# Seven beginnings within a 64-byte line for the split weights of a two-block network on one core

## The chip, the core and the metric

The kernel runs on one core of a Trainium2 chip. The metric is device time in microseconds (us) of one execution, all weights being read from HBM; the run before was timed three times.

## The reference

Two networks run one after the other on 256 tokens of width 1024, in float32. The first has four layers (a gated mixer with a causal convolution of 31 taps, an attention with 16 heads and forget gates, a mixer with a convolution of 3 taps, and the first kind again). The second has two layers, each with a two-branch attention and a feed-forward part of width 2 x 2816. What matters here is that nearly all of the work has this form:

```python
def conv_ffn(h, w_up, conv_w, conv_b, w_down):
    u = h @ w_up
    ...
    return (jax.nn.silu(g) * val) @ w_down
```

A matrix of activations (256 tokens) is multiplied by a large matrix of weights that is used once. The other mixers (`h @ w_in`, `... @ w_out`) are the same product with other nonlinear steps between.

## The kernel before, in words

**Weights.** A weight matrix comes in tiles of 128 x 1024 float32 (512 KB). `need` (L684, called for every tile) starts the DMA into a buffer `wr` and then makes two tiles of it: ScalarE writes `wh`, the value rounded to the type fp32r, and VectorE writes `wl = wr - wh`, the rest. Activations are split in the same way, into `hh` and `hl` (eight chunks of 128 x 256, kept for a layer) or into `ph` and `pl` (one chunk each).

**Products.** `mm3` makes one float32 product from three matmuls in fp32r: `wh` by `hh`, `wh` by `hl`, `wl` by `hh`. The weights are the stationary operand (128 x 128, a LDWEIGHTS of its own before each matmul), the activations the moving one (256 columns). `dense` does this for eight chunks into half a PSUM bank `pd`, `pair` for two such halves; `Out` accumulates the second matrix of a mixer into four banks `po`. `tokens512` turns the operands round: there `wh` and `wl` move (512 columns) and the activations stay. Tiles of the kind "native" are not split: they are multiplied from `wr` in plain float32.

**Order.** `Graph.schedule` plays the whole program through with costs for each instruction, and writes down on which engine and in which order everything is issued. It also gives each buffer its slot: five for `wr`, six for `wh`, seven for `wl`, in rotation. `place` (L467 to L481) then makes the tile of a slot; every tile is padded to a multiple of 128 bytes (LINE), and three small unused tiles (PHASES) set off the pools.

**Addresses.** In the built program the pools lie so that every tile begins 32 bytes into a 64-byte line of SBUF: `hh` at byte 29856 of each partition, `wr0` at 64608, `wh0` at 85088, `wl0` at 89184, `ph0` at 197024, and all other slots a multiple of 64 bytes behind these. A slice of 128 columns of weights, or of one chunk of activations, is 512 or 1024 bytes further, so each LDWEIGHTS and each matmul begins at 32 within its line, too.

Of the kernel before, what the change touches and what calls it, by code (L numbers as in the profile page):

```python
# [18 lines left out]
LINE = 128  # L19

PHASES = {"const": 8, "weights": 16, "big": 16}
WIDTH = {F32: 4, F32R: 4, I32: 4, BF: 2}
DEBUG = []

# [100 lines left out]
class Graph:  # L125
# [341 lines left out]
    def place(self, pool, b, tag):  # L467

        size = WIDTH[b.dtype]
        n, line = int(np.prod(b.shape[1:])), LINE // size  # L470
        if b.pool == "psum" or n % line == 0:
            return pool.tile(b.shape, b.dtype, name=b.name, tag=tag, bufs=1)
        t = pool.tile([b.shape[0], -(-n // line) * line], b.dtype, name=b.name, tag=tag, bufs=1)[:, :n]
        names = [f"a{i}" for i in range(len(b.shape) - 1)]
        if len(names) == 1:
            return t
        return t.rearrange(f"p ({' '.join(names)}) -> p {' '.join(names)}", **dict(zip(names[1:], b.shape[2:])))


    def issue(self, tc, ctx, pools):  # L480
        nc = tc.nc  # L481
        ctx.enter_context(tc.manual_schedule())
        made = {n: ctx.enter_context(tc.tile_pool(name=n, bufs=1, **kw)) for n, kw in pools.items()}
        for n, w in PHASES.items():
            made[n].tile([128, w], F32, name="phase_" + n, tag="phase", bufs=1)
# [1363 lines left out]
```

## Time and profile before

| | |
|---|---|
| time, median of 3 runs | 1811.41 us (1805.84 to 1814.57) |
| profiled execution: its own time | 1812.58 us |
| profiled execution: its span | 1810.8 us |
| TensorE matmul busy | 1792.4 us (99%) |
| TensorE weight load busy | 1722.9 us (95%) |
| VectorE busy | 1483.2 us (82%) |
| ScalarE busy | 1102.9 us (61%) |
| GpSimd busy | 363.6 us (20%) |
| DMA, mean rate | 185 GB/s |

Matmuls overlap, and a matmul's duration in the trace (280 ns) is the time from its start until its result is there. The pace of a row of matmuls is read from their starts, not from their durations: in the chain of waits, where a piece gives the count of matmuls and the time that they took together, or in the timeline, which gives the start of each.

### The profile page before, as it was taken

Reading aid. Unit: us, or ns where it says so; the run is one execution under the profiler, and the core shown is the slowest. Engines: PE = TensorE matmul, PEld = TensorE weight load, DVE = VectorE, ACT = ScalarE, POOL = GpSimd, SP = SyncE. Lnnn points to the kernel's source line nnn. Section 1 sums busy time; section 2 is a strip of 40 time slices with the busy share of each in tenths; the row PEclk is TensorE's granted clock in tenths of the full one; section 3 lists DMA queues with packets and bytes.
Section 4 is the critical chain, followed back from the end, with each engine's and each line's share of the span. In section 5 each row is a group of like instructions: output and inputs, shape, how many; then the busy total and the mean of one; then the engine's idle time right before and its main releaser. Section 6 shows DMA issues by size and latency. Waiting matters only on the chain.

```text
span 1810.8 us, 37129 instructions
## 1 busy us (share of the span) xinstructions
PE 1792.4 (99%) x14088; PEld 1722.9 (95%) x14088; DVE 1483.2 (82%) x3264; ACT 1102.9 (61%) x1975; POOL 363.6 (20%) x462
## 2 busy tenths in 40 slices
PE   9999999999999999999999999999999999999998
PEld 8999998999999999999999989999999989999998
DVE  7999998777787777689998897889998675687676
ACT  6786665554554444477767469665556468765554
POOL 3997311000010000069953000010001000000001
PEclk9999999999999999999999999999999999999999
DMA  6445666776747655444465756658884433446561
GB/s 219 151 139 188 187 217 197 254 250 226 241 146 223 177 174 174 152 128 142 151 196 184 238 175 204 207 177 279 274 271 127 163 126 119 136 157 209 187 187 48
DMA packets 107171, 334.90 MB, mean 185 GB/s; under 512 B 12784, under 2 KB 13168, under 8 KB 106992
## 3 DMA queue, kind: packets, MB, share of 16 engines
q1 hardware_dynamic: 106992, 332.52, 57.1%
q8 instruction: 111, 1.82, 0.4%
q14 instruction: 68, 0.56, 0.1%
HBM read 331.43 MB, written 1.05 MB: 184 GB/s over the span
## 4 chain that ended last, share of the span: by engine, by line
PE 88%; DVE 6%; DMA 3%; ACT 2%; issue 1%; POOL 0%; SPq 0%; ACTq 0%; DVEq 0%; POOLq 0%
PE pd L512 59%; PE po L512 21%; PE pa L512 8%; DMA wa<-in_w_ada 2%; DVE wl L512 1%; PE idle L512 1%; DVE wa L512 1%; ACT L512 0%; ACT wh L512 0%; DVE x L512 0%; DMA wr<-in_a_in 0%; DVE hn L512 0%; DVE IQ L512 0%; DVE hh L512 0%; DVE nm L512 0%
## 5 line engine op out<-in xcount | busy, mean ns | idle before, releaser
L512 ACT ACTIVATE wh<-wr 128x1024 fp32r<-128x1024 f32 x466 | 489.4, 1056 | 401.1 <-PE pd L512 257.0
L512 DVE TENSOR_TENSOR wl<-wr,wh 128x1024 fp32r<-128x1024 f32 x466 | 574.9, 1241 | 126.9 <-ACT wh L512 124.4
L512 PE MATMUL pd<-hh,wh 128*128 128x256 f32 x2360 | 670.0, 286 | 3.0 <-DVE up L512 2.1
L512 PE MATMUL pd<-hl,wh 128*128 128x256 f32 x2360 | 660.8, 283 | 0.2 <-DVE hl L512 0.2
L512 PE MATMUL pd<-hh,wl 128*128 128x256 f32 x2360 | 660.2, 283 | 0.0
L512 PEld LDWEIGHTS pd<-hh,wh 128*128 128x128 f32 x2360 | 445.5, 189 | 5.8 <-ACT wh L512 2.0
L512 PEld LDWEIGHTS pd<-hl,wh 128*128 128x128 f32 x2360 | 443.1, 189 | 1.6 <-issue 0.5
L512 PEld LDWEIGHTS pd<-hh,wl 128*128 128x128 f32 x2360 | 443.4, 189 | 1.2 <-issue 0.5
L512 POOL TENSOR_TENSOR C<-C,tap 128x230 f32<-128x230 f32 (+16 forms) x366 | 269.0, 758 | 47.0 <-ACT tap L512 35.2
L512 PE MATMUL po<-ph,wh 128*128 128x256 f32 x904 | 250.4, 282 | 0.0
L512 PE MATMUL po<-ph,wl 128*128 128x256 f32 x904 | 249.2, 281 | 0.0
L512 PE MATMUL po<-pl,wh 128*128 128x256 f32 x904 | 238.6, 281 | 0.1
L512 DVE SCALAR_TENSOR_TENSOR po<-U,vec,po 128x255 f32<-128x255 f32 (+19 forms) x530 | 216.4, 471 | 2.2
L512 PE MATMUL pd<-hn,wr 128*128 128x256 f32 x960 | 214.7, 381 | 0.0
L512 PEld LDWEIGHTS pd<-hn,wr 128*128 128x128 f32 x960 | 179.8, 190 | 23.0
L512 PEld LDWEIGHTS po<-ph,wh 128*128 128x128 f32 x904 | 169.8, 188 | 0.7 <-ACT ph L512 0.3
L512 PEld LDWEIGHTS po<-ph,wl 128*128 128x128 f32 x904 | 170.1, 188 | 0.0
L512 ACT ACTIVATE tap<-U,vec 128x226 f32<-128x226 f32 (+17 forms) x366 | 155.3, 479 | 17.3 <-POOL C L512 8.1
L512 PEld LDWEIGHTS po<-pl,wh 128*128 128x128 f32 x904 | 162.8, 188 | 0.4 <-DVE pl L512 0.3
L512 POOL TENSOR_TENSOR sq<-sq 128x256 f32<-128x256 f32 x16 | 13.6, 850 | 443.7 <-ACT sq L512 443.1
L512 POOL TENSOR_TENSOR r<-r,neghalf 128x4 f32<-128x4 f32 (+1 forms) x22 | 28.8, 1309 | 298.4 <-DVE r L512 258.4
L512 DVE CUSTOM_DVE_ANT_0 wa<-wa,scr,mods 128x512 f32<-128x512 f32 x96 | 72.1, 751 | 14.1 <-DMA wa<-in_w_ada 13.5
(272 smaller groups left out, 2502.1 us busy)
## 6 DMA issues: line engine op xcount, KB each, us to landing
wr<-in_a_in SPq DMA_DIRECT2D x96, 512.0 KB, 3.6
wa<-in_w_ada SPq DMA_DIRECT2D x192, 256.0 KB, 3.8
wr<-in_w_up SPq DMA_DIRECT2D x88, 512.0 KB, 4.3
wr<-in_c_in SPq DMA_DIRECT2D x64, 512.0 KB, 3.6
wr<-in_m_in SPq DMA_DIRECT2D x64, 512.0 KB, 4.3
wr<-in_b_in SPq DMA_DIRECT2D x48, 512.0 KB, 4.5
wr<-in_w_dn SPq DMA_DIRECT2D x44, 512.0 KB, 4.2
wr<-in_a_out SPq DMA_DIRECT2D x32, 512.0 KB, 4.4
```

The lines of the kernel that those rows point to most:

```text
L512: getattr(eng[o.eng], o.fn)(*args, **kw)
```

## The change

`place` gives the slots of `wh` and `wl` a beginning of their own. A table SHIFT names the number of float32 elements by which the tile's first element is moved behind the slot's first byte: 8, 10, 12, 14, 2, 4 for the six slots of `wh`, and the same with a 6 at the end for the seven slots of `wl`. The slot itself becomes 128 bytes longer, so the slot that follows begins at 32 within its line again.

```diff
+SHIFT = {"wh": (8, 10, 12, 14, 2, 4), "wl": (8, 10, 12, 14, 2, 4, 6)}
...
-        if b.pool == "psum" or n % line == 0:
+        turn = SHIFT.get(b.tag)
+        at = turn[b.slot % len(turn)] if turn else 0
+        if b.pool == "psum" or n % line == 0 and not at:
             return pool.tile(b.shape, b.dtype, name=b.name, tag=tag, bufs=1)
-        t = pool.tile([b.shape[0], -(-n // line) * line], b.dtype, name=b.name, tag=tag, bufs=1)[:, :n]
+        t = pool.tile([b.shape[0], -(-(n + at) // line) * line], b.dtype, name=b.name, tag=tag, bufs=1)[:, at:at + n]
```

In the built program the tiles begin at these bytes of a 64-byte line:

| slot | 0 | 1 | 2 | 3 | 4 | 5 | 6 |
|---|---|---|---|---|---|---|---|
| `wh`, before | 32 | 32 | 32 | 32 | 32 | 32 | |
| `wh`, changed | 0 | 8 | 16 | 24 | 40 | 48 | |
| `wl`, before | 32 | 32 | 32 | 32 | 32 | 32 | 32 |
| `wl`, changed | 0 | 8 | 16 | 24 | 40 | 48 | 56 |

All other tiles (`wr`, `hh`, `hl`, `ph`, `pl`, x and the rest) still begin at 32. No instruction is added, dropped or moved: on each of the five engines the list of instructions, with what each waits for, is the same as before but for the line numbers, and each slot holds the same tiles.

## Rows read from the trace of the kernel before

**Rows 1.** The page: busy time by engine; granted clock in 40 slices; the chain's shares.

```profile
PE 1792.4 (99%) x14088; PEld 1722.9 (95%) x14088; DVE 1483.2 (82%) x3264; ACT 1102.9 (61%) x1975; POOL 363.6 (20%) x462
...
PEclk9999999999999999999999999999999999999999
...
PE 88%; DVE 6%; DMA 3%; ACT 2%; issue 1%; POOL 0%; SPq 0%; ACTq 0%; DVEq 0%; POOLq 0%
PE pd L512 59%; PE po L512 21%; PE pa L512 8%; DMA wa<-in_w_ada 2%; DVE wl L512 1%; PE idle L512 1%; DVE wa L512 1%; ACT L512 0%; ACT wh L512 0%; DVE x L512 0%; DMA wr<-in_a_in 0%; DVE hn L512 0%; DVE IQ L512 0%; DVE hh L512 0%; DVE nm L512 0%
```

**Rows 2.** Matmul groups: out<-moving,stationary, shapes, count, busy us, mean ns, idle before.

```profile
L512 PE MATMUL pd<-hh,wh 128*128 128x256 f32 x2360 | 670.0, 286 | 3.0 <-DVE up L512 2.1 <-ACT hh L512 0.8
...
L512 PE MATMUL po<-ph,wh 128*128 128x256 f32 x904 | 250.4, 282 | 0.0
...
L512 PE MATMUL po<-hh,wh 128*128 128x256 f32 x184 | 51.3, 279 | 0.0
...
L512 PE MATMUL pd<-wh,hh 128*128 128x512 f32 x80 | 32.7, 411 | 0.0
...
L512 PE MATMUL pd<-ph,wh 128*128 128x256 f32 x72 | 21.2, 295 | 1.2 <-DVE qm L512 0.8 <-ACT hn L512 0.2
```

**Rows 3.** Chain in both feed-forward parts: start us, us, what, count.

```profile
1246.48 5.65 PE pd L512 x48
1252.14 2.83 PE po L512 x24
...
1638.30 5.65 PE pd L512 x48
1643.95 2.83 PE po L512 x24
```

**Rows 4.** Chain from 942 us, output matrix of the fourth layer.

```profile
942.30 8.28 PE po L512 x72
...
950.71 34.06 PE po L512 x300
```

**Rows 5.** Timeline of TensorE around 988 us: start us, duration us, matmul.

```profile
987.78 0.28 PE L512 MATMUL pd<-hl,wh 128*128 128x256 f32 x1
...
988.12 0.28 PE L512 MATMUL pd<-hl,wh 128*128 128x256 f32 x1
...
989.04 0.28 PE L512 MATMUL pd<-hh,wl 128*128 128x256 f32 x1
...
989.40 0.28 PE L512 MATMUL pd<-hh,wl 128*128 128x256 f32 x1
```

**Rows 6.** Timeline of weight loads: eight for matmuls of one column.

```profile
1015.85 0.97 PEld L512 LDWEIGHTS pa<-cst,sq 128*128 128x128 f32 x8
```

**Rows 7.** Busy us (and count) by stretch: PE, PEld, DVE, ACT, POOL, clock, DMA.

```profile
945.00:975.00 30.00, 30.00 (x268) 29.96 (x267) 29.95 (x49) 21.16 (x34) 13.20 (x12) 1.00 0.69 207
1240.00:1350.00 110.00, 110.00 (x937) 110.00 (x936) 101.70 (x203) 62.89 (x91) 0.00 (x0) 1.00 0.87 281
...
1640.00:1760.00 120.00, 120.00 (x1021) 120.00 (x1020) 84.92 (x128) 66.23 (x100) 0.00 (x0) 1.00 0.60 188
```

**Rows 8.** Timeline: first and last of 18 matmuls with 512 moving columns.

```profile
239.01 0.40 PE L512 MATMUL pd<-wh,rawl 128*128 128x512 f32 x1
...
243.21 0.40 PE L512 MATMUL pd<-wh,rawl 128*128 128x512 f32 x1
```

**Rows 9.** Groups of VectorE and ScalarE, columns as in rows 2.

```profile
L512 DVE TENSOR_TENSOR wl<-wr,wh 128x1024 fp32r<-128x1024 f32 x466 | 574.9, 1241 | 126.9 <-ACT wh L512 124.4 <-DMA wr<-in_w_b 0.4
...
L512 DVE SCALAR_TENSOR_TENSOR y<-u,vec,y 128x255 f32<-128x255 f32 x16 | 7.7, 484 | 0.5
L512 DVE SCALAR_TENSOR_TENSOR y<-u,vec,y 128x254 f32<-128x254 f32 x16 | 7.7, 483 | 0.5
...
L512 ACT ACTIVATE tap<-U,vec 128x226 f32<-128x226 f32 x32 | 15.1, 472 | 0.5 <-DVE U L512 0.2 <-POOL C L512 0.2
...
L512 ACT ACTIVATE tap<-U,vec 128x236 f32<-128x236 f32 x16 | 7.6, 478 | 0.0
```

## The prediction

> **What bounds the kernel now.** I read the page first. TensorE is busy for 99% of the span at the full clock (every slice of the clock line is a 9), and the chain of waits lies on TensorE for 88%: 59% on `pd`, 21% on `po` [rows 1]. So the pace of the matmuls is the time, and everything else feeds it. The groups tell which matmuls these are. There are 2360 + 904 + 184 + 72 = 3520 triples of fp32r matmuls with 256 moving columns and split weights, 10,560 in all [rows 2] (each row is one of three with the same count).
>
> Next comes their pace. In both feed-forward parts the chain repeats one piece: 48 matmuls into `pd` in 5.65 us, 24 into `po` in 2.83 us [rows 3]. That is 8.48 us for 72, or 117.8 ns from start to start, alike at 1246 us and at 1638 us. VectorE is busy for 101.7 of 110 us in the first of these stretches and for 84.9 of 120 in the second, and DMA engines for 0.87 and 0.60 of the time [rows 7]; the pace does not move with it. 10,560 x 117.8 ns = 1244 us is 69% of the span, nearly the whole of the chain's share on `pd` and `po` less the unsplit tiles.
>
> The row that matters most is the exception. In the output matrix of the fourth layer 300 such matmuls take 34.06 us, 113.5 ns each [rows 4], while VectorE is busy for 29.95 of 30 us [rows 7]. The fast pace ends at 988.2 us with no idle time: three matmuls take 0.34 us just before (987.78 to 988.12), and 0.36 us soon after (989.04 to 989.40) [rows 5], the same kind of matmul on buffers that all begin at byte 32. So at equal addresses there are two stable paces, 113.5 and 117.8 ns, 4.3 ns apart, and what decides is how the streams of TensorE happen to stand to each other in time. I put the matmuls at the fast pace at some 700 (400 from 942 to 988 us, the rest in pieces of 10 to 90), so 9,860 go at the slow one.
>
> A third row gives a floor. Eight weight loads for matmuls of one column take 0.97 us together, the last 0.19 us of it its own duration [rows 6]: (0.97 - 0.19) / 7 = 111.4 ns from load to load. No split matmul can go faster, because each brings a load of the same 128 columns.
>
> **The change part by part.** No instruction and no wait is added, so the change can only alter durations. There are four places where it could.
>
> *Weight loads* (two in three from `wh`, one in three from `wl`). All 10,560 matmuls load from a tile whose beginning moves against that of the moving tile, by seven amounts, and never by none. The trace has no load that begins elsewhere than at 32, so its cost is bounded from both sides. Best, every matmul goes at the floor: 117.8 - 111.4 = 6.4 ns on 9,860 and 2.1 ns on 700, 65 us. The nearest row on that side is the fast pace: 9,860 x 4.3 ns = 42 us. Worst, I allow one step of the same size upward, since 4.3 ns is the only step that the trace shows: 10,560 x 4.3 ns = 45 us lost. I take the middle between the two measured paces, 2.15 ns on 9,860, 21 us gained. The reason is that the slow pace is a standing that returns to itself triple after triple while all beginnings are alike. Now `wh` and `wl` rotate through six and seven beginnings, so the standing differs from tile to tile (every 8 triples), and the two known paces are what it can fall into. Why not all at the fast pace: a standing that suits one beginning need not suit the next.
>
> *Matmuls with moving weights.* Of these there are 240 in the shape of rows 2, and 48 more. Eighteen take 4.20 us, 233.3 ns each [rows 8]. Twice the step above would be 288 x 8.6 ns = 2.5 us either way; I take 0.
>
> *Splitting.* VectorE and ScalarE now write and read tiles that begin elsewhere: 466 subtractions of 1241 ns [rows 9] and as many copies. Instructions whose operands begin 4 or 8 bytes further are there: 255 elements in 484 ns and 254 in 483; on ScalarE 226 elements in 472 ns and 236, begun 40 bytes earlier in the row, in 478 [rows 9]. This is 0.6 to 1 ns per element and no step at any beginning, so I take 0. Were it 5 ns on each of the 466 pairs, it would be 2.3 us on each engine, hidden where VectorE has 35 of 120 us free, not in the stretch from 945 us where it has none [rows 7].
>
> *Longer slots.* 13 x 128 bytes push `wa` and the pools behind; all still begin at 32, so 0.
>
> How much of a faster pace reaches the end? In the second feed-forward part all of it: VectorE has 84.9 of 120 us of work. In the first it has 101.7 of 110 us, 92%; a pace 4% faster still leaves TensorE last. Around 945 us VectorE is full. In the convolution layers short waits between matmuls will take some. I count 0.9 of the gain: 21 x 0.9 = 19 us. The sum against the profiled execution is 1812.6 - 19 = 1793.6 us. That execution is 1.2 us above the median of the three runs, so against the median it is 1792; I say 1793.
>
> **Rivals.**
>
> *All at the fast pace or below.* If equal beginnings are what makes the slow standing possible, it vanishes: 42 x 0.9 = 38 us, 1774; with the floor as the end, 65 us, 1747. For it: one stretch of 300 holds the fast pace over 12 tiles. Against it: that stretch shows that equal beginnings do not exclude the fast pace, so they are not the whole cause.
>
> *The places do not matter.* Two paces at equal addresses can be read as a proof that addresses are not the cause: the standing is set by the last interruption, and so it stays. Then the slow pace keeps its 117.8 ns, and the time is 1811, with 9 us either way for the luck of the interruptions. The Trainium skill, "SBUF — State Buffer", section on the two separate sides, says that TensorE's port waits for no other engine. The rows agree (the same 117.8 ns under light and heavy VectorE load), but two streams of TensorE itself are not other engines. By that rule the change is worth nothing.
>
> *Slower.* A load that begins at an odd multiple of 8 bytes may cost more. This holds for three of six `wh` slots and four of seven `wl` slots, so for 2/3 x 3/6 + 1/3 x 4/7 = 52% of the loads. The place is the load under the running matmul, the price one step of 4.3 ns: 0.52 x 10,560 x 4.3 ns = 24 us, 1836. With all seven it is 45 us, 1858. It decides as soon as the load ends after the matmul that covers it; with 111.4 ns from load to load against 117.8 the room is 6.4 ns, and at the fast pace only 2.1 ns. For it: so little room. Against it: no row shows a dearer beginning on any engine. The Trainium skill, "SBUF — State Buffer", specifications, speaks against the change here: SBUF is read in lines of 16 bytes, and each crossing into a new line costs. A load begun in mid-line crosses one line more; no run here shows that.
>
> **How the numbers follow.** Half a step faster (1793): 0.36. Fast pace everywhere or below (1747 to 1780): 0.11. No effect (1802 to 1820): 0.25. Slower (1820 to 1858): 0.28. Hence faster by over 0.5% 0.46 (0.01 of the first case falls short of it), same 0.26, slower 0.28; 0.5%, 9 us, is about what a measurement of this kernel can tell from no change. The likeliest case alone spans 1778 to 1802. Leaving out half of the second case and a little over a third of the last gives 1768 to 1838 for 8 in 10.
>
> **What would show it.** The chain's pieces of 48 and 24 in the feed-forward parts: 5.55 and 2.77 us in the forecast, with differing pieces from tile to tile; 5.45 and 2.72 at the fast pace throughout; 5.65 and 2.83 if nothing happens; over 5.75 if the odd beginnings cost. The subtraction should stay at 1241 ns. The forecast is wrong if the pace within one tile's 24 matmuls leaves the band from 113 to 118 ns, or if the pace falls and the span does not, because VectorE then sets the end.

## The result, and the profile after

The changed kernel takes 1816.59 us (median of nine runs, 1814.04 to 1818.68), the kernel before in the same runs 1807.54 us (1801.2 to 1814.57). The ratio is 1.0054 (95% interval 1.0031 to 1.0077): slower by half a per cent, where 1793 us and a gain were forecast. The time lies in the range of 1768 to 1838 us; the direction is wrong.

The page after: busy time by engine, and the shares of the chain of waits by engine.

```profile
span 1816.1 us, 37129 instructions
...
PE 1801.2 (99%) x14088; PEld 1733.4 (95%) x14088; DVE 1483.4 (82%) x3264; ACT 1103.0 (61%) x1975; POOL 362.2 (20%) x462
...
PEclk9999999999999999999999999999999999999999
...
PE 91%; DVE 4%; DMA 3%; ACT 1%; issue 1%; POOL 0%; SPq 0%; ACTq 0%; DVEq 0%; POOLq 0%
```

Against [rows 1] TensorE's times have moved: 1792.4 to 1801.2 us of matmuls and 1722.9 to 1733.4 us of weight loads. VectorE (1483.2 to 1483.4) and ScalarE (1102.9 to 1103.0) stand still. The medians differ by 9 us. The two profiled executions, 1812.58 and 1817.94 us, differ by less: the span grows by 5.3 us (1810.8 to 1816.1), the matmul time by 8.8 us, and 3.5 us of TensorE's idle time are gone (18.4 to 14.9 us), as the chain's share on VectorE falls from 6 to 4%. No engine waits for something new; the matmuls have a slower pace.

The clock has to be looked at, too. A 9 in the clock line means 90% or more of a slice, so it is not the full clock throughout, as the prediction read it. One stretch of the kernel before, columns as in [rows 7]:

```profile
1000.00:1006.00 6.00, 6.00 (x29) 6.00 (x30) 2.27 (x6) 0.69 (x1) 1.80 (x1) 0.50 0.96 336
```

Here the granted clock is 0.50, the lower of its two levels (1.2 GHz). Apart from the program's last 15 us there are four such stretches before, 20 us together, and six after, 27 us; elsewhere it is 1.00 (2.4 GHz). Of the 7 us more at half clock at most half, 3.4 us, can be time lost in the profiled execution after. The clock is not the result, though: over the runs it is the same on the mean, 0.993 in the nine of the change and in the 31 of the kernel before that were timed beside pad_only, and the paces below are taken without the triples at half clock.

The chain of the second feed-forward part and of the fourth layer's output matrix after: start us, us, what, count.

```profile
942.68 8.65 PE po L516 x72
...
951.46 35.59 PE po L516 x300
...
1633.66 5.69 PE pd L516 x48
1639.35 2.84 PE po L516 x24
1642.19 5.67 PE pd L516 x48
1647.86 2.83 PE po L516 x24
1650.69 5.71 PE pd L516 x48
1656.39 2.83 PE po L516 x24
```

Two things have changed. Where before nearly every piece was 5.65 and 2.83 us [rows 3], the pieces now differ from tile to tile and lie a little above: here 5.67 to 5.71 and 2.83 to 2.84, in the first feed-forward part 5.61 to 5.70 and 2.82 to 2.88. And the fast stretch of [rows 4], 300 matmuls in 34.06 us, takes 35.59 us, 118.6 ns each: the fast pace is gone.

The same can be said of all matmuls with split weights. I took the starts of every triple of them with nothing between (9,715 in each trace) and left out some 260 with a wait or at half clock. Before, 7.5% of the triples took 342 ns or less (the fast pace, 113.3 ns a matmul) and the others 117.79 ns a matmul, on the mean 117.45. After, 0.1% are fast and the mean is 118.16. The difference on 10,560 matmuls, 0.71 ns each, is 7.5 us. Half of it (0.075 x 10,560 x 4.9 ns = 3.9 us) is the fast pace that ended, the other half (0.925 x 10,560 x 0.37 ns = 3.6 us) a dearer slow pace. Each share is that of one profiled execution; the one before lies above the median of its kernel (1812.58 against 1807.54 us), so its usual share of the fast pace may be larger, which no run shows.

The groups of the split after: count, then busy us and mean ns of one, and idle time before.

```profile
L516 DVE TENSOR_TENSOR wl<-wr,wh 128x1024 fp32r<-128x1024 f32 x466 | 575.3, 1242 | 129.0 <-ACT wh L516 125.0 <-DMA wr<-in_b_v 0.8 <-DMA wr<-in_w_a 0.4
...
L516 ACT ACTIVATE wh<-wr 128x1024 fp32r<-128x1024 f32 x466 | 490.6, 1059 | 405.1 <-PE pd L516 253.5 <-PE po L516 71.7 <-issue 51.8
```

The subtraction takes 1242 ns against 1241 [rows 9], the copy 1059 against 1056 in the trace before: on the mean, VectorE and ScalarE do not mind where the tile begins.

### The profile page after: what moved, and what is told of

Its sections match the earlier page's. It is cut to its first block, busy times and chain, and to the rows that moved or that the text cites. A ratio compares the mean times of both kernels' runs of the same rounds, so it can differ in the third digit from the quotient of the medians.

```text
span 1816.1 us, 37129 instructions
## 1 busy us (share of the span) xinstructions
PE 1801.2 (99%) x14088; PEld 1733.4 (95%) x14088; DVE 1483.4 (82%) x3264; ACT 1103.0 (61%) x1975; POOL 362.2 (20%) x462
## 4 chain that ended last, share of the span: by engine, by line
PE 91%; DVE 4%; DMA 3%; ACT 1%; issue 1%; POOL 0%; SPq 0%; ACTq 0%; DVEq 0%; POOLq 0%
PE pd L516 59%; PE po L516 22%; PE pa L516 8%; DMA wa<-in_w_ada 2%; PE idle L516 1%; DVE wl L516 1%; DVE wa L516 1%; DMA wr<-in_b_in 1%; DMA wr<-in_a_in 0%; ACT wh L516 0%; DVE IQ L516 0%; DVE nm L516 0%; DVE x L516 0%; DVE hd L516 0%; DVE m L516 0%
## 5 line engine op out<-in xcount | busy, mean ns | idle before, releaser
L516 ACT ACTIVATE wh<-wr 128x1024 fp32r<-128x1024 f32 x466 | 490.6, 1059 | 405.1 <-PE pd L516 253.5
L516 DVE TENSOR_TENSOR wl<-wr,wh 128x1024 fp32r<-128x1024 f32 x466 | 575.3, 1242 | 129.0 <-ACT wh L516 125.0
```

The lines of the kernel that those rows point to most:

```text
L516: getattr(eng[o.eng], o.fn)(*args, **kw)
```

## Experiments

Each kernel was timed beside runs of the kernel before on the same chip; ratios are to these. "Pace" is the mean over the triples described above, "fast" the share of triples at 342 ns or less. Two measures of a place are needed. One is the byte at which a tile begins in its 64-byte line, 32 in the kernel before. The other is the distance: how far the moving tile (`hh`, `hl`, `ph`, `pl`) begins behind the weights, counted within 256 bytes. In the kernel before all weights begin at 96 within 256 bytes and all moving tiles at 160, so every distance is 64. All kernels have the same instructions (14,088 matmuls each); only addresses differ. Their mean granted clock lies between 0.9915 and 0.9942; the slowest kernel, d0, has the highest and mix_all64, one of the three fastest, the lowest, so the clock does not order them.

| kernel | ratio (95%) | pace, ns | fast |
|---|---|---|---|
| before | 1 | 117.45 | 7.5% |
| the change | 1.0054 (1.0031 to 1.0077) | 118.16 | 0.1% |
| pad_only | 0.9964 (0.9945 to 0.9982) | 116.46 | 38.5% |
| wh_only | 1.0060 (1.0032 to 1.0087) | 118.17 | 0.1% |
| wl_only | 1.0027 (1.0011 to 1.0042) | 117.57 | 2.7% |
| all_0 | 1.0063 (1.0042 to 1.0084) | 118.43 | 0% |
| all_40 | 1.0043 (1.0024 to 1.0063) | 118.20 | 0% |
| all_48 | 1.0023 (1.0005 to 1.0042) | 117.87 | 0% |
| shift_256 | 1.0012 (0.9992 to 1.0031) | 117.82 | 0% |
| d0 | 1.0124 (1.0090 to 1.0158) | 119.89 | 0% |
| d128 | 1.0076 (1.0053 to 1.0100) | 118.93 | 0% |
| d192 | 0.9936 (0.9906 to 0.9966) | 115.36 | 53.8% |
| mix | 0.9849 (0.9812 to 0.9886) | 113.74 | 90.6% |
| mix_seven | 1.0067 (1.0047 to 1.0087) | 118.42 | 0% |
| mix_w16 | 1.0088 (1.0057 to 1.0119) | 118.84 | 0% |
| mix_all16 | 1.0020 (1.0000 to 1.0040) | 117.69 | 1.4% |
| mix_all32 | 0.9863 (0.9832 to 0.9893) | 113.76 | 90.2% |
| mix_all64 | 0.9884 (0.9857 to 0.9911) | 113.78 | 89.9% |

### The longer slots alone

```diff
-SHIFT = {"wh": (8, 10, 12, 14, 2, 4), "wl": (8, 10, 12, 14, 2, 4, 6)}
+SHIFT = {"wh": (0,) * 6, "wl": (0,) * 7}
...
-        if b.pool == "psum" or n % line == 0 and not at:
+        if b.pool == "psum" or n % line == 0 and not turn:
...
-... [b.shape[0], -(-(n + at) // line) * line] ...
+... [b.shape[0], (-(-(n + at) // line) + (1 if turn else 0)) * line] ...
```

This is pad_only: the slots stay 128 bytes longer, nothing is shifted in them.

> The slots of wh and wl are 128 bytes longer, as in the change, but nothing is shifted: all tiles begin at 32 within their 64-byte line. Theory A (what costs is that the beginnings differ from slot to slot): the two paces of before, 117.8 and 113.3 ns, and nothing between; 1803 to 1812 us. Theory C (the distance between the slots costs, not the beginning within the line): a spread of paces around 118.2 ns as in the changed kernel, and 1813 to 1819 us.

1803.79 us, 0.4% faster than before: in theory A's range, though not with its two paces alone. Chain of the second feed-forward part in this kernel, and its output matrix of the fourth layer.

```profile
946.71 34.06 PE po L516 x300
...
1620.93 5.70 PE pd L516 x48
1626.63 2.73 PE po L516 x24
1629.37 5.68 PE pd L516 x48
1635.04 2.73 PE po L516 x24
```

The pieces into `po` run at the fast pace (2.73 / 24 = 113.8 ns), those into `pd` slower than before (5.70 / 48 = 118.8). All tiles still begin at 32 within the line, but the distances have changed. Each `wl` but the last of the seven now lies 128 bytes off its `wh` within 256, and 13 x 128 = 1664 = 6.5 x 256 bytes push `ph` and `pl` by another 128. So `pd` (from `hh`, `hl`) has distances of 64 to `wh` and 192 to these `wl`, and `po` (from `ph`, `pl`) the reverse. The step "longer slots: 0" is wrong, and from here to the whole change (1.0054 / 0.9964) the seven places cost 0.9%, not 0.5%.

### One place for all slots

```diff
-SHIFT = {"wh": (8, 10, 12, 14, 2, 4), "wl": (8, 10, 12, 14, 2, 4, 6)}
+SHIFT = {"wh": (8,) * 6, "wl": (8,) * 7}
```

This is all_0; all_40 has 2 and all_48 has 4 in place of 8, and the slots are 128 bytes longer as in the change.

> Every wh and wl begins at 0, the moving tiles stay at 32. Theory A (beginnings that differ from slot to slot cost): an orderly pace again, one or two values for all tiles, 113.3 to 117.8 ns; 1775 to 1812 us. Theory B (each beginning, against that of the moving tile, has a pace of its own): the pace that the changed kernel's tiles have where both wh and wl begin at 0, 118.4 to 119.0 ns; 1816 to 1824 us.

> Every wh and wl begins at 40, an odd multiple of 8 bytes. Theory A: an orderly pace of 113.3 to 117.8 ns, 1775 to 1812 us. Theory B: the pace of the changed kernel's tiles with both at 40, 118 to 119 ns; 1812 to 1822 us. Theory D (an odd multiple of 8 is dear by itself): slower than with all at 48 by 4.3 ns a matmul at the most, 1830 to 1855 us.

> Every wh and wl begins at 48. Theory A: an orderly pace of 113.3 to 117.8 ns, 1775 to 1812 us. Theory B: the pace of the changed kernel's tiles with both at 48, 117.7 ns in eight of nine and no stretch at 113.3; 1808 to 1814 us.

1819.99, 1815.62 and 1813.35 us, as theory B had it: each loses against the longer slots alone, none has a fast triple, though all slots begin alike. Differing from slot to slot is therefore not what makes the change slow; a beginning that does not suit the moving tile is enough. The rival of odd multiples of 8 bytes falls as well: with byte 40, an odd multiple, the pace is 118.20 ns, no dearer than the 118.43 with byte 0, and 0.3 ns, not 4.3, above the 117.87 with byte 48.

### The seven places with slots of another length

```diff
-... [b.shape[0], -(-(n + at) // line) * line] ...
+... [b.shape[0], (-(-(n + at) // line) + (1 if turn else 0)) * line] ...
```

> The change's seven beginnings, but each slot of wh and wl is 256 bytes longer instead of 128, so that slots stand to each other, and the pools behind to them, as before in steps of 256 bytes. Theory A (the beginnings within the line cost, whatever the slot's length): the spread of paces of the changed kernel, 118.0 to 118.5 ns on average, no stretch at 113.3; 1812 to 1820 us. Theory C (the longer slots made the loss): the paces of before, 1803 to 1811 us.

This is shift_256: 1812.29 us, 1.0012 with 1 in the interval. Each slot of `wh` and `wl` is one line of 128 bytes longer still; 256 bytes more for each leave the distances as they were before but for the seven shifts. The fast triples go from 7.5% to 0, as theory A had it, but the others stay at 117.8 ns, below its 118.0. The other half of the change's loss, the dearer slow pace, thus comes only with the 128 bytes by which `wl` and the later pools move.

### The distance alone

```diff
-PHASES = {"const": 8, "weights": 16, "big": 16}
+PHASES = {"const": 8, "weights": 32, "big": 64}
```

This is d0; d128 has 64 and 32, d192 has 48 and 48. Only the unused tiles differ from the kernel before: weights begin 64, 192 or 128 bytes later, still at 32 within the line, and the moving tiles at the same place within 256 bytes. The name gives the distance; before it is 64.

> As d192, but the weight pool 64 bytes further than before: moving tile and weight at the same place within 256 bytes. Theories E and F give no number for it but another pace than 117.8 or another share of 113.3; 1765 to 1830 us. Theory G: 1803 to 1811 us.

> No shift and no longer slots. The pool of weights lies 128 bytes further, the moving tiles where they were, so that a moving tile stands 192 instead of 64 bytes past a weight tile, counted within 256 bytes. Theory E (what decides between 113.3 and 117.8 ns is where moving tile and weight stand to each other within 256 bytes, and wl counts like wh): 113.3 ns nearly everywhere, 1762 to 1775 us. Theory F (the place of wl against wh decides as well): two paces as before, 113.3 and 117.7, about half of each as in pad_only for ph with the seventh wl slot (48%); 1780 to 1800 us. Theory G (addresses beyond the 64-byte line do not matter): 1803 to 1811 us.

> All begin at 32, no longer slots; moving tile and weight 128 bytes apart within 256 bytes, wh and wl alike. The distances measured so far gave 120.0 (0), 117.8 with 7% fast (64) and 117.7 with 54% fast (192). If the pace changes smoothly with the distance, 128 lies between 64 and 192: 116 to 117.5 ns, 1797 to 1808 us. If distances of whole 128 bytes are bad by themselves, about 120 ns as at 0: 1825 to 1833 us.

1829.84, 1796.98 and 1822.73 us. Chain of d0 in the second feed-forward part:

```profile
1641.28 5.76 PE pd L512 x48
1647.04 2.88 PE po L512 x24
1649.92 5.76 PE pd L512 x48
1655.68 2.88 PE po L512 x24
```

With weights and moving tile at the same place within 256 bytes these matmuls take 120.0 ns (5.76 / 48; 119.89 on the mean of all), the slowest pace of all runs and as regular as before. So with equal beginnings it is not chance alone that decides: the distance changes the pace. Theory G falls with all three, and theory E with d192, where little more than half of the triples are fast, as theory F had it. d128 lies in neither of its two ranges, and its pace, 118.93 ns, not between those of 64 and 192.

### Both distances, and the change on top

```diff
-PHASES = {"const": 8, "weights": 16, "big": 16}
+PHASES = {"const": 8, "weights": 48, "big": 112}
+SHIFT = {"wl": 32}
...
+        at = SHIFT.get(b.tag, 0)
+        if at:
+            return pool.tile([b.shape[0], n + 64], ...)[:, at:at + n]
```

In mix the distance is 192 for `wh` and 64 for `wl`, everywhere (in the longer slots alone only `po` has it, with six of the seven `wl`); all tiles begin at 32.

> All begin at 32 within 64 bytes. Within 256 bytes wh stands at 224, wl at 96 and every moving tile at 160: the standing in which pad_only ran ph's matmuls at 113.3 ns for 79% of the time. Theory F: 113.3 ns for some 80% of all split matmuls, mean 114.1 ns against 117.45 before, 35 us less: 1768 to 1778 us. Theory E: half of the loads favourable, 1785 to 1795 us. Theory G: 1803 to 1811 us.

1780.91 us, 1.5% under the kernel before and 2.0% under the change (0.9849 / 1.0054). That is nearest to theory F: the share of the fast pace is above its 80%, the time 3 us above its range. Its page, busy time and the chain's shares by engine:

```profile
PE 1760.1 (99%) x14088; PEld 1688.6 (95%) x14088; DVE 1478.1 (83%) x3264; ACT 1103.3 (62%) x1975; POOL 363.9 (20%) x462
...
PE 84%; DVE 8%; ACT 3%; DMA 3%; issue 1%; POOL 0%; SPq 0%; ACTq 0%; DVEq 0%; POOLq 0%
```

And its chain in the second feed-forward part:

```profile
1614.95 5.44 PE pd L517 x48
1620.39 2.72 PE po L517 x24
1623.11 5.44 PE pd L517 x48
1628.55 2.72 PE po L517 x24
```

5.44 / 48 = 113.3 ns, piece after piece, in both feed-forward parts. The pace gains 3.71 ns x 10,560 = 39 us, TensorE is busy for 32 us less, and the time falls by 27 us (0.0151 x 1808; the spans of the two profiled executions differ by 29.7 us). The chain's share on VectorE rises from 6 to 8% and on ScalarE from 2 to 3%: some of the gain ends in waits for them.

mix_seven puts the change's seven places on this:

```diff
-SHIFT = {"wl": 32}
+SHIFT = {"wh": (8, 10, 12, 14, 2, 4), "wl": (40, 42, 44, 46, 34, 36, 38)}
...
-        at = SHIFT.get(b.tag, 0)
+        turn = SHIFT.get(b.tag)
+        at = turn[b.slot % len(turn)] if turn else 0
```

> The layout of mix with the change's seven beginnings added to it. Theory H: no triple at 113.3 ns, mean pace about 118, 1806 to 1818 us: the change then costs 25 to 35 us against mix, where it cost 9 against the kernel before. Theory I: most of the fast pace stays, 1780 to 1795 us.

1819.41 us. Its chain:

```profile
1634.42 5.71 PE pd L518 x48
1640.12 2.84 PE po L518 x24
1642.96 5.67 PE pd L518 x48
1648.63 2.83 PE po L518 x24
```

These are pieces like those of the change, and theory H holds, with a time just above its range. From 0.9849 to 1.0067 the same seven places cost 2.2%, while they cost 0.9% on the longer slots and nothing that can be measured on the distances of before (shift_256). So the seven places cost what their base had of the fast pace: 90.6%, 38.5% and 7.5% of the triples.

### The place in the line

```diff
-SHIFT = {"wl": 32}
+SHIFT = {"wh": 4, "wl": 36}                                              # mix_w16
+SHIFT = {"wh": 4, "wl": 36, "c_hh": 4, "c_hl": 4, "ph": 4, "pl": 4}      # mix_all16
```

mix_all32 and mix_all64 move the same tiles as mix_all16 by 8 and by 16 elements. In mix_w16 the weights alone begin 16 bytes further; in the others the moving tiles do, too, so each distance is that of mix.

> The layout of mix, with every wh and wl 16 bytes further and the moving tiles where they were: the distance is no longer a multiple of 64 bytes. Theory H (the fast pace needs moving tile and weight to begin at the same place within a line of 64 bytes): no triple at 113.3 ns, mean pace 117.5 to 118.5, 1806 to 1818 us. Theory I (only the standing within 256 bytes counts, in steps much coarser than 16 bytes): 80% or more at 113.3 ns, 1776 to 1788 us.

> The layout of mix with weights and moving tiles (hh, hl, ph, pl) all 16 bytes further: every distance is that of mix, but all begin at 48 within their line. Theory H (distance counts): as mix, 80% or more at 113.3 ns, 1776 to 1788 us. Theory J (the place within the line counts by itself, and 32 is a good one): the fast pace goes, 1806 to 1818 us.

> As mix with all six kinds of tiles begun 32 bytes further: every distance stays, all begin at byte 0 of a 64-byte line. Theory A (byte 32 of the line is needed): the fast pace is lost as with 16 bytes, 1805 to 1820 us. Theory C (a raster of 32 bytes is what is needed; 16 bytes missed it): as mix, 1775 to 1787 us, pieces of 48 in 5.44 us.

> The kernel mix (wh 192 and wl 64 bytes from the moving tile, counted within 256; 1781 us) with wh, wl, hh, hl, ph and pl all begun 64 bytes further: every distance stays, and all still begin at byte 32 of a 64-byte line. Theory A (distances decide, if all begin at 32 within the line): as mix, 1775 to 1787 us, pieces of 48 in 5.44 us. Theory B (the place within 256 bytes itself decides, the distances only by it): the fast pace is lost, 1800 to 1825.

1822.21, 1812.70, 1781.35 and 1784.61 us: no fast triple in mix_w16, which is slower still than theory H had it; theory J for mix_all16, C for mix_all32, A for mix_all64. One piece of the chain of mix_all16, and one of mix_all32:

```profile
1649.96 5.65 PE pd L520 x48
```

```profile
1644.18 5.44 PE pd L520 x48
```

Moved together by 32 or 64 bytes, the tiles keep the fast pace; moved together by 16 they fall to 117.7 ns, at the same distances. So two things count: all operands begin at a multiple of 32 bytes (as far as 16, 32 and 64 bytes tell), and the distances are good ones, those of mix best. The first alone is not enough (all_0, d0, d128 have no fast triple). The Trainium skill, "SBUF — State Buffer", specifications, gives lines of 16 bytes, each crossing of which costs. By that rule mix_all16 would equal mix, since all its tiles begin at a multiple of 16. It does not (1812.70 against 1780.91 us); the raster (the step of addresses) that counts here is 32 bytes.

### Half of the change

```diff
-SHIFT = {"wh": (8, 10, 12, 14, 2, 4), "wl": (8, 10, 12, 14, 2, 4, 6)}
+SHIFT = {"wh": (8, 10, 12, 14, 2, 4), "wl": (0,) * 7}     # wh_only
+SHIFT = {"wh": (0,) * 6, "wl": (8, 10, 12, 14, 2, 4, 6)}  # wl_only
...
-        if b.pool == "psum" or n % line == 0 and not at:
+        if b.pool == "psum" or n % line == 0 and not turn:
...
-... [b.shape[0], -(-(n + at) // line) * line] ...
+... [b.shape[0], (n + line) if turn else -(-n // line) * line] ...
```

> The longer slots, and of the change only the six beginnings of wh; wl begins at 32. Theory 1 (each load that begins elsewhere in the line costs by itself; two loads in three are from wh): two thirds of the 13 us from longer slots alone (1803.8) to the whole change (1816.6), 1812. Theory 2 (the fast pace needs all three operands at 32; one that is off ends it for the whole triple): all of it, 1815 to 1818, with no stretch at the fast pace. Theory 3 (only wl is sensitive): 1804.

> The longer slots, and of the change only the seven beginnings of wl; wh begins at 32. Theory 1 (cost by load, one in three from wl): a third of the 13 us, 1808. Theory 2 (one operand that is off ends the fast pace for the whole triple): 1813 to 1818, with no stretch at the fast pace. Theory 3 (only wh is sensitive): 1804.

1817.18 and 1811.44 us, against 1803.79 for the longer slots alone: 1.0% and 0.6%, together more than the 0.9% of both. So the cost does not add up by loads, and theory 2 fits best, though wl_only keeps a few fast triples and lies under its range. Either half takes nearly all fast triples (38.5% to 0.1% and to 2.7%), since each triple needs `wh` and `wl`, and once it is gone the other half has little left to take. Of the change's places one in six of `wh` and one in seven of `wl` is a multiple of 32 (byte 0).

## Why the prediction was wrong

**What bounds the kernel: right.** The pace of the matmuls is the time. After the change the matmul time of the profiled execution is 8.8 us up and the median 9 us; in mix 32 us less of matmuls are 27 us less.

**Weight loads: the step that failed.** It read the slow pace as "a standing that returns to itself triple after triple while all beginnings are alike", so that seven beginnings would break it. The runs show the reverse. The fast pace is the one that needs its places (a raster of 32 bytes for all operands, and the distances), and beginnings off them end it: 38.5% of the triples in pad_only and 90.6% in mix become 0.1% and 0 with the seven places. [rows 4] were read the wrong way round: 300 matmuls at the fast pace at beginnings all at 32 were the only row on what that pace needs, and the change takes just that away from five in six `wh`.

Two facts of the argument still hold. The places alone do not settle which pace a stretch takes: in d192, at the same distances, the pieces of the first feed-forward part all take 5.44 us (from 1225 to 1345 us) and those of the second, but for its first, 5.65. And a pace lasts until something stops it: of the 19 fast stretches in the trace before, 18 end where a matmul of another kind comes between. The last is the one that the prediction saw end at 988.2 us "with no idle time" [rows 5]. Around this time there stand, in the kernel before (start us, duration us):

```profile
987.78 0.40 ACT L512 ACTIVATE hh<-hn 128x256 fp32r<-128x256 f32 x1
...
988.01 0.19 PEld L512 LDWEIGHTS pd<-hl,wh 128*128 128x128 f32 x1
...
988.23 0.19 PEld L512 LDWEIGHTS pd<-hh,wh 128*128 128x128 f32 x1
...
988.23 0.39 PE L512 MATMUL pd<-hh,wh 128*128 128x256 f32 x1
988.46 0.40 PE L512 MATMUL pd<-hh,wl 128*128 128x256 f32 x2
```

The load at 988.23 comes 0.22 us after the one before, twice a pace, and its matmul takes 0.39 us instead of 0.28. The signal that this load waits for is one of ScalarE, which had just ended a chunk of `hh` (987.78 + 0.40 = 988.18). So a wait of 0.1 us for ScalarE ended the fast stretch, though TensorE counts as busy.

**The size of a middle value.** Half a step was taken on 9,860 matmuls because two paces were known. There are more: 113.3, 117.7 to 117.8, 118.8 and 120.0 ns appear, by distance. The prediction's sign of being wrong came true: pieces of 24 in 2.84 us are 118.3 ns, outside its band of 113 to 118 ns.

**Longer slots: wrong.** "All still begin at 32, so 0" looked at the line of 64 bytes alone. The slots moved `wl` against `wh` and `ph` against both by 128 within 256 bytes, and by themselves gained 0.4%. The front part's list of addresses would have shown it: the place within 64 bytes was worked out for each tile, the place within 256 was not.

**Splitting and moving weights: right.** The subtraction takes 1242 ns against 1241. Matmuls with 512 moving columns that follow each other start 233.2 ns apart before and 233.1 after.

**How much reaches the end.** 0.9 of a gain in pace was counted. mix has nearly the gain in pace that the first rival priced (42 us at the fast pace throughout); of its 39 us, 27 came through, 0.7 (0.76 by the profiled executions). The rows on VectorE in the prediction (101.7 of 110 us busy) point to it: its share of the chain has grown.

**The rivals.** "All at the fast pace": the wrong condition, yet the right size; mix is that case, 1781 against 1774. (Its other figure, 1747, leaves out the 0.9; 65 x 0.9 = 58 us would give 1754.) "Places do not matter" forecast 1811 with 9 us either way, which holds the changed kernel's time by chance; d0 and mix, 1829.84 and 1780.91 us from moved beginnings alone, refute it. The sentence of the Trainium skill that was set beside it, "SBUF — State Buffer", section on the two separate sides, tells of other engines and is not touched. Another sentence of the Trainium skill, "TensorE: Matmul & The Clock Gate", step-by-step part, says that loading the next tile's weights takes no SBUF bandwidth from the running matmul. These runs speak against it: if the two streams never met, d0 and mix should have one pace, and they have 120.0 and 113.3 ns. That it is bandwidth is not shown. "Slower" had the right sign with the wrong place (odd multiples of 8) and a price of 24 us where 7.5 us of pace were lost.

**What stays open.** Why 32 bytes and why these distances: the runs show that the pace depends on both, not which part of the chip makes it so; nor what makes a row of matmuls settle on one pace or the other where both occur. That weight load and moving stream meet in the same part of SBUF fits d0 being the slowest; nothing here shows it. Distances that are no multiple of 64 were tried only together with other beginnings, and of the mixed pairs only 192 with 64 and, in the longer slots, 64 with 192.

## What to carry over

Where a row of matmuls with a weight load each sets the time, the addresses of stationary and moving tiles are a parameter: print them, begin all of them at a multiple of 32 bytes, as here, and try a few offsets of the pools against each other within 256 bytes; here this moved the time from 1830 to 1781 us with not one instruction changed. A change that pads a buffer shifts everything behind it, so time the padding alone before judging what it was for. A 9 in a line of tenths, and a busy engine, can hide a stretch at half clock or a wait: look into the stretch. When a trace shows a rare better state, first ask what allows it, then whether the change keeps that.

## What the runs showed of the hardware

- Fp32r matmuls with 256 columns and a weight load each have a pace that depends on addresses: 120.0 ns at distance 0 (119.9 on the mean), 118.9 on the mean at 128, 117.8 (7.5% at 113.3) at 64, 117.7 (53.8% at 113.3) at 192, and 113.3 (90.6%) at 192 for one weight tile and 64 for the other.
- The fast pace is kept when all operands move by 32 or 64 bytes (1781.35 and 1784.61 us) and lost when they move by 16 (1812.70).
- A weight load that waits 0.1 us for another engine leaves no idle time in TensorE's row: its matmul shows 0.39 us instead of 0.28 (at 988.23 us before).
- VectorE and ScalarE take the same time, on the mean, on tiles that begin at the change's seven places as at byte 32 (1242 against 1241 ns, 1059 against 1056 ns).
